# Where the gate and up weights lie in SBUF: one offset for every split buffer, and other homes for three blocks

## The chip, the core and the metric

The kernel runs on one core of one Trainium2 chip. The metric is the device time of the whole kernel in microseconds, the median of several executions. Engines are called as in the profile: PE is the matrix engine (PEld its weight loads), DVE the vector engine, ACT the scalar engine, POOL the general one and SP the one that issues most transfers.

## What is computed

One layer of a hybrid decoder on 512 tokens of width 1024, in float32. Two token mixers (a gated linear recurrence and a sparse attention with three branches) share one input projection, and a sandwich-normed feed-forward and a gated input embedding follow. The part that matters here is the feed-forward's first half:

```python
h = rmsnorm(x, norm_ffn_pre[i])
gate, up = jnp.split(h @ ffn_w_gate_up[i], 2, axis=-1)          # h: 512 x 1024, weights: 1024 x 5632
x = x + rmsnorm((jax.nn.silu(gate) * up) @ ffn_w_down[i], norm_ffn_post[i])
x = x + jax.nn.sigmoid(x @ ple_w_gate[i] + ple_b_gate[i]) * (p[i] @ ple_w_proj[i])
```

## The kernel before

**Products.** A float32 product is made of three matmuls on rounded operands: every operand is split into a high part (a cast on ACT) and a low part (a subtraction on DVE), and `three` adds high x high, high x low and low x high in one PSUM bank. The normed tokens lie transposed in `aTh` and `aTl`, 8 slices of 128 rows by 512 tokens. For every matmul PE loads a stationary operand of 128 x 128 and streams a moving one past it, and the load of the next one runs while the present one streams.

**The gate and up stage.** The 2816 columns of gate and of up are cut into 22 blocks of 128 (`NF`). A block needs its gate weights and its up weights, 128 x 1024 values each, as a high and a low tile. There are three forms.

- Blocks 0 and 1 (`first`) run in two halves of 256 tokens, because the last tokens are still being normed and transposed (`to_T`, L254 and L255). The up weights of block 1 have tiles of their own, `UP1`; the other three pairs lie in `whf` and `wlf`.
- Blocks 2, 3 and 4 (up to `SF` = 5) are plain: `gu_load` loads and splits, `gu_mm` runs 24 matmuls of 512 tokens for gate into bank `mm` and 24 for up into bank `sc`, `gu_act` applies the SiLU (L1224), multiplies (L1225), and splits and stores what the down-projection needs.
- Blocks 5 to 21 (`s_block`) use seven half-size products instead of eight, on sums of tokens (T1, T3, T2, T4, made once in `t_sums` while blocks 2 to 4 run, L1302 to L1312) and sums of weights (`s_load`, L1348 and L1349 for the splits). Each has seven stretches of 12 matmuls of 256 tokens: two with gate weights, two with w12, two with w34 and one with the high half of the up weights, vw. The weights of the first six lie in `whf` and `wlf`, those of the last in `vwh` and `vwl`, whose low part is finished by an adding transfer from POOL's queue (L1358).

**The buffers.** The pool `wp2` holds three loaded tiles (`rawf`), three `whf` and three `wlf`, used in turn. `wtile` cuts a tile of 1024 floats out of a buffer of 1024 + `STEP` floats, and small tiles named pad lie between the groups. SBUF is laid out in the order in which the tiles are first named, so a pad of n floats moves all that follows by 4n bytes. The pool `ff` opens behind it in the space of the out-projection's weights (`wo`) and norms, and holds a home for each tile of the feed-forward: `a0` to `a5` and `s0` to `s10` for the activations, the sums, w12 and w34, and `vwh`, `vwl`. A home can be written once whatever lay in its bytes, or in the same home before, was read for the last time. The weights that the attention stage reads are in another pool, opened and closed earlier; the attention pool `attn` begins with homes (`KS0` to `pc`), behind which small tiles and the scores' exponentials `e` follow; PE transposes `e` with the identity as the moving operand (`tr<-ident,e`).

**Order.** PE's matmuls keep the program's order in this stage (`strict`). The order of the other engines' instructions is set when the program is built, by priorities and estimated times; `wload` gives its load, cast and subtraction a priority of 100 places ahead (`AHEAD`). Each engine then runs its queue in that order, and an instruction that waits holds up those behind it.

Of the kernel before, what the change touches and what calls it, by code (L numbers as in the profile page):

```python
# [8 lines left out]
F32 = mybir.dt.float32  # L9
F32R = mybir.dt.float32r  # L10
# [6 lines left out]
S, D, KT, TT = 512, 1024, 8, 4  # L17
# [18 lines left out]
VP = (4,)  # L36

SF = 5
STEP = 16
SA = 160  # L40
WARM = 13
PTB = 3
# [2 lines left out]
def f32(ap):  # L45
    return ap.bitcast(F32)
# [3 lines left out]
def layer_kernel(ctx, tc, a, out):  # L50
# [14 lines left out]
    def nm(s):  # L65
        uid[0] += 1
        return f"{s}{uid[0]}"

    def bank(tag, shape=None):
        return ps.tile(shape or [128, 512], F32, tag=tag, name=nm(tag), bufs=PB[tag])  # L70
# [8 lines left out]
    def wraw(src, shape, w, ahead=None):  # L79
        raw = wpool[0].tile(shape, F32, tag="raw" + w, name=nm("raw"), bufs=WB[w][0])  # L80
        with tc.high_priority(offset=AHEAD if ahead is None else ahead):
            nc.sync.dma_start(raw, src)
        return raw

    def wtile(tag, shape=(KT, 128), dt=F32R):

        v = wpool[0].tile([128, KT * 128 + STEP], dt, tag=tag, name=nm(tag), bufs=WB["f"][1])[:, :KT * 128]
        return v.rearrange("p (k c) -> p k c", k=shape[0])

    def wload(src, shape, w, hl=None):  # L90

        raw = wraw(src, shape, w)
        h, l = hl or [wtile(x + w) for x in ("wh", "wl")]
        with tc.high_priority(offset=AHEAD):
            nc.scalar.copy(h, raw)
            nc.vector.tensor_sub(l, raw, f32(h))
        return h, l
# [654 lines left out]

    KS, QS, PTc, E, ATT = {}, {}, {}, {}, {}
    for tag, n, bufs in (("KS0", 4 * S, 1), ("KS1", 4 * S, 1), ("KS2", 4 * S, 1), ("QS", S, 6), ("PT", 2 * S, PTB),
                         ("pc", 2 * S, 1)):
        ap_.tile([128, n], F32, tag=tag, name=nm("home"), bufs=bufs)

    def k_epi(j, br):
# [307 lines left out]


    wpool[0] = ctx.enter_context(tc.tile_pool(name="wp2", bufs=2, reuse_waits="tile"))
    for tag, n, bufs in (("rawf", 1024, 3), ("pad0", 8, 1), ("whf", 1024 + STEP, 3), ("pad1", 16, 1),
                         ("wlf", 1024 + STEP, 3), ("pad2", 8, 1)):  # L1070
        wpool[0].tile([128, n], F32, tag=tag, name=nm("home"), bufs=bufs)
    late = ctx.enter_context(tc.tile_pool(name="late", bufs=1, reuse_waits="tile"))
# [79 lines left out]
            post1(t, 0, YP[t])  # L1152
    wgu = a["ffn_w_gate_up"][0].rearrange("(k p) c -> p k c", p=128)

    def gu_load(f, up=None):
        return (wload(wgu[:, :, f * 128:(f + 1) * 128], [128, KT, 128], "f"),
                wload(wgu[:, :, DFF + f * 128:DFF + (f + 1) * 128], [128, KT, 128], "f", up))

    with tc.issue_after(WO["dma", 3].ins):
        first = [gu_load(0)]  # L1160
# [8 lines left out]
    for ch in (1,):  # L1169
        ws = WO[ch]  # L1170
        for t in range(TT):
            p_ = bank(("pv", "mq")[t % 2])
            tl = slice(t * 128, (t + 1) * 128)
            three(p_, [(aTh[:, k, tl], aTl[:, k, tl], ws[k // 2][0][:, k % 2], ws[k // 2][1][:, k % 2])
                       for k in range(KT)],
                  {TK[0]: turn_0, TK[1]: turn_1} if t == TT - 1 else {})
            post1(t, ch, p_)
            resid(t, og, sss)
            norm2_sum(t)
            if t != 2:  # L1180
                norm2(t)
            if t == 1:
                first.append(gu_load(1, UP1))
# [19 lines left out]
    def gu_mm(w, banks, cs, then=None):  # L1203
        for i, ((wh, wl), p_) in enumerate(zip(w, banks)):
            three(p_[:, cs], [(wh[:, k], wl[:, k], aTh[:, k, cs], aTl[:, k, cs]) for k in range(KT)],
                  {TK[2]: then} if i == 1 and then else {})
# [45 lines left out]
    ff = ctx.enter_context(tc.tile_pool(name="ff", bufs=1, reuse_waits="tile"))  # L1252
# [3 lines left out]
    for j in range(NJ2):  # L1256
        if j == NJ2 - 1:
            for t_, n in (("t1", 8), ("t3", 8), ("t2", 8), ("tm", 4), ("w12", 4), ("w34", 4)):
                ff.tile([128, n * HS], F32, tag=t_, name=nm("home"))
            ff.tile([128, 56], F32, tag="pad0", name=nm("pad"))  # L1260
            for t_ in ("vwh", "vwl"):
                ff.tile([128, 2 * HS], F32, tag=t_, name=nm("home"), bufs=2)
            ff.tile([128, 8], F32, tag="pad1", name=nm("pad"))
        if j % 2 == 0:
            ff.tile([128, len(BLK[j // 2]), 2, HS], F32, tag=f"a{j // 2}", name=nm("home"))
        ff.tile([128, 2, 2, HS], F32, tag=f"s{j}", name=nm("home"))
# [22 lines left out]
    def t_sums(step):  # L1289

        if step == 0:
            SB["tmp"] = [home(t_, [128, half, HS], F32) for t_ in ("s8", "s9")]
        n_ = ("T1", "T3", "T2", "T4")[step]
        SB[n_] = part_of(0, 1)
        if step < 3:
            t_ = home(n_.lower(), [128, 2, half, HS])
            SB[n_] = t_[:, 0], t_[:, 1]
        x, z = SB["tmp"]
        lo1, lo2, hi1, hi2 = ([f32(v) for v in part_of(a_, b_)] for a_ in range(2) for b_ in range(2))

        def cut(n_, v):
            nc.scalar.copy(SB[n_][0], v)  # L1302
            nc.vector.tensor_sub(SB[n_][1], v, f32(SB[n_][0]))

        def diff(o_, t_, p_, q_):
            nc.vector.tensor_sub(o_, p_[0], q_[0])
            nc.vector.tensor_sub(t_, p_[1], q_[1])
            nc.vector.tensor_add(o_, o_, t_)

        def minus(o_, v, q_):  # L1310
            nc.vector.scalar_tensor_tensor(o_, v, -1.0, q_[0], op0=OP.mult, op1=OP.subtract)
            nc.vector.tensor_sub(o_, o_, q_[1])  # L1312

        if step == 0:
            diff(x, z, lo1, lo2)
            cut("T1", x)
        elif step == 1:
            diff(z, x, hi2, lo2)
            cut("T3", z)
        elif step == 2:  # L1320
            minus(x, z, lo1)
            cut("T2", x)
            minus(z, x, hi1)
        else:
            cut("T4", z)
# [54 lines left out]
    def s_block(f):  # L1380
        gw, w12, w34, vw = s_load(f)
        X, Z, W = (bank(t_)[:, :HS] for t_ in ("mm", "sc", "tr"))
        if f == SF:
            SB["tmp"] = home("tm", [128, half, HS], F32)
        P1, P5, U2, U3 = (SB["tmp"][:, i] for i in range(half))

        def times(p_, w, at, b, fresh=False):
            for k in range(half):
                for n_, (u, m_) in enumerate(((0, 0), (0, 1), (1, 0))):
                    mm(p_, w[u][:, at + k], b[m_][:, k], start=fresh and k == 0 and n_ == 0,  # L1390
                       stop=k == half - 1 and n_ == 2, skip_group_check=not fresh)

        def act(st, o_):
            times(X, gw, 0, part_of(0, 0), True)
            nc.scalar.copy(P1, X)
            times(W, gw, half, part_of(1, 0), True)
            nc.vector.tensor_add(st[:, :HS], W, P1)
            times(X, w12, half, SB["T2"])
            nc.scalar.copy(U2, X)
            times(Z, w12, 0, SB["T1"], True)  # L1400
            last["P5"] = nc.scalar.copy(P5, Z)
            times(X, w34, 0, SB["T3"])
            last["U3"] = nc.scalar.copy(U3, X)
            times(Z, w34, half, part_of(1, 1))
            nc.vector.tensor_add(st[:, HS:], Z, U2)
            last["silu"] = tab(nc.scalar.activation(st, st, AF.Silu))
            times(X, vw, 0, SB["T4"])
            nc.vector.tensor_add(U3, U3, P5)
            nc.vector.scalar_tensor_tensor(o_[:, :HS], X, -1.0, st[:, :HS], op0=OP.mult, op1=OP.mult)
            last["o2"] = nc.vector.scalar_tensor_tensor(o_[:, HS:], U3, -1.0, st[:, HS:], op0=OP.mult, op1=OP.mult)  # L1410

        gu_act(f, act, None)

    strict[0] = True
    for f in range(2, NF):
        if f - 2 <= SF - 2:
            t_sums(f - 2)
        if f >= SF:
            s_block(f)
            continue  # L1420
        w, banks = gu_load(f), (bank("mm"), bank("sc"))
        gu_mm(w, banks, slice(0, S))
        gu_act(f, *banks)

# [71 lines left out]
    for b, js in enumerate(BLK):  # L1496
        n, end = len(js), b == len(BLK) - 1
# [152 lines left out]
    for b, js in enumerate(BLK):  # L1650
        w, s4 = ws.pop(b)
# [115 lines left out]
```

## Time and profile before

| what | value |
|---|---|
| median of 3 executions | 896.84 us (896.24 to 896.94) |
| the profiled execution's own time | 896.88 us |
| its span from first to last instruction | 895.1 us |
| PE busy | 884.7 us, 99% |
| DVE busy | 705.4 us, 79% |
| ACT busy | 557.1 us, 62% |
| POOL busy | 161.1 us, 18% |
| gate and up stage, first to last matmul | 495.79 to 724.13 us of the span |

In the profile's groups, a line gives the operation, the tile written, the tiles read, and the shape. Matmuls overlap in the records: a matmul of 512 columns is shown as some 0.39 us long and one of 256 as 0.28, while the next one begins earlier; what a matmul costs in a dense stretch is the distance from its start to the next one's. L107 is the helper that issues every matmul, so tiles and start times tell the matmuls apart. In a timeline, a row is a start, a length, the engine, the line, the operation, the tiles, the shape and the number of instructions merged. In the chain of waits a row is a start, a length and what ran.

### The profile page before, as it was taken

The numbers are of one execution on the slowest core, as the hardware profiler recorded it, in microseconds if no ns is written. First come the engines' busy times: TensorE is split into PE (matmuls) and PEld (weight loads), VectorE is DVE, ScalarE is ACT, GpSimd is POOL, SyncE is SP. The second block draws the span as 40 slices with busy tenths as digits, with TensorE's granted clock in tenths as the row PEclk, the third lists the DMA queues.
The fourth block names the chain that finished last, engine by engine and source line by source line (L and its number), as shares of the span: only waits on it lengthen the run. The fifth ranks groups of instructions, "written<-read, shape, count | busy, mean of one in ns | idle before, by whom it ended". The sixth has DMA issues, their size and how long they took to land.

```text
span 895.1 us, 14187 instructions
## 1 busy us (share of the span) xinstructions
PE 884.7 (99%) x5111; PEld 761.9 (85%) x5111; DVE 705.4 (79%) x1366; ACT 557.1 (62%) x1072; POOL 161.1 (18%) x247
## 2 busy tenths in 40 slices
PE   8999999999999999999999999999999999999998
PEld 6977888878888888888888988999999988878887
DVE  6657786968788788787848589888888898898852
ACT  6468958666677667767736345676667664466520
POOL 4101201214143232323402100111111100002000
PEclk9999999999999999999999999999999999999999
DMA  9433435282114111111048244666667675558511
GB/s 299 98 95 98 115 95 165 74 162 71 41 44 107 48 48 48 47 48 48 26 140 258 94 123 125 147 164 166 151 146 182 159 222 192 191 181 245 189 59 48
DMA packets 138934, 110.94 MB, mean 124 GB/s; under 512 B 6936, under 2 KB 119664, under 8 KB 138864
## 3 DMA queue, kind: packets, MB, share of 16 engines
q1 hardware_dynamic: 126272, 95.61, 36.2%
q0 software_dynamic: 12576, 14.42, 8.1%
q8 instruction: 40, 0.66, 0.3%
q14 instruction: 30, 0.25, 0.1%
q10 hardware_dynamic: 16, 0.00, 0.0%
HBM read 97.96 MB, written 8.91 MB: 119 GB/s over the span
## 4 chain that ended last, share of the span: by engine, by line
PE 90%; DVE 5%; ACT 2%; issue 1%; DMA 1%; SPq 1%; POOL 0%; DVEq 0%; ACTq 0%
PE mm L107 47%; PE sc L107 19%; PE mq L107 7%; PE tr L107 6%; PE pv L107 5%; PE tr L110 4%; DVE wl L169 1%; DMA y<-in_w_in_dram 1%; DVE PT L953 1%; DVE e L862 1%; ACT e L865 1%; DVE aTl L1441 1%; PE sc L110 0%; ACT wh L168 0%; DVE QS L783 0%
## 5 line engine op out<-in xcount | busy, mean ns | idle before, releaser
L107 PE MATMUL mm<-aTh,wh 128*128 128x512 f32 x344 | 140.4, 408 | 0.0
L107 PE MATMUL mm<-aTh,wl 128*128 128x512 f32 x344 | 134.7, 392 | 0.0
L107 PE MATMUL mm<-aTl,wh 128*128 128x512 f32 x344 | 134.5, 391 | 0.0
L877 POOL TENSOR_SCALAR e<-e,sm 128x128 f32<-128x128 f32 (+3 forms) x128 | 78.8, 632 | 152.8 <-DVE sm L873 102.2
L169 DVE TENSOR_TENSOR wl<-raw,wh 128x1024 fp32r<-128x1024 f32 x59 | 73.5, 1249 | 25.6 <-ACT wh L168 21.1
L865 ACT ACTIVATE e<-e,mn 128x128 f32<-128x128 f32 (+3 forms) x128 | 71.5, 559 | 28.4 <-DVE mn L862 18.2
L168 ACT CAST wh<-raw 128x1024 fp32r<-128x1024 f32 x59 | 61.7, 1047 | 26.6 <-PE mm L107 23.7
L107 PEld LDWEIGHTS mm<-aTh,wl 128*128 128x128 f32 x344 | 64.6, 188 | 14.2
L107 PEld LDWEIGHTS mm<-aTh,wh 128*128 128x128 f32 x344 | 64.7, 188 | 12.9 <-issue 3.4
L107 PEld LDWEIGHTS mm<-aTl,wh 128*128 128x128 f32 x344 | 64.9, 189 | 9.4
L862 DVE CUSTOM_DVE_ANT_0 e<-sc,toep 128x128 f32<-128x128 f32 (+3 forms) x128 | 59.8, 484 | 16.0 <-PE sc L107 15.2
L953 DVE TENSOR_TENSOR PT<-tr,PT 128x512 fp32r<-128x512 f32 x96 | 56.6, 596 | 15.6 <-ACT PT L952 15.0
L952 ACT CAST PT<-tr 128x512 fp32r<-128x512 f32 x96 | 47.9, 512 | 24.5 <-PE tr L110 23.4
L1349 DVE TENSOR_TENSOR wlf<-T,whf 128x1024 fp32r<-128x1024 f32 x34 | 41.6, 1224 | 22.9 <-ACT whf L1348 22.9
L107 PE MATMUL sc<-KS,QS 128*128 128x512 f32 (+2 forms) x192 | 54.1, 364 | 0.1
L107 PE MATMUL mm<-T,whf 128*128 128x256 f32 x272 | 50.1, 282 | 0.0
L110 PE MATMUL tr<-ident,e 128*128 128x128 f32 x320 | 48.6, 272 | 0.0
L110 PEld LDWEIGHTS tr<-ident,e 128*128 128x128 f32 x320 | 39.9, 141 | 9.2 <-DVE PT L953 0.3
L107 PEld LDWEIGHTS mm<-T,whf 128*128 128x128 f32 x272 | 41.8, 188 | 0.0
L107 PE MATMUL mm<-T,aTh 128*128 128x512 f32 (+1 forms) x144 | 40.6, 367 | 0.0
L107 PEld LDWEIGHTS sc<-KS,QS 128*128 128x128 f32 x192 | 33.8, 188 | 7.9 <-issue 1.4
L1348 ACT CAST whf<-T 128x512 fp32r<-128x512 f32 x68 | 38.5, 616 | 1.5 <-PE sc L107 1.5
(462 smaller groups left out, 2507.1 us busy)
## 6 DMA issues: line engine op xcount, KB each, us to landing
raw<-in_w_in_dram SPq DMA_DIRECT2D x48, 512.0 KB, 3.8
raw<-in_ffn_w_gate_up_dram SPq DMA_DIRECT2D x44, 512.0 KB, 4.2
raw<-in_ffn_w_down_dram SPq DMA_DIRECT2D x25, 512.0 KB, 4.4
rd<-r POOLq DMA_DIRECT2D x11, 512.0 KB, 3.9
w<-in_ffn_w_gate_up_dram POOLq DMA_DIRECT2D x17, 256.0 KB, 5.2
raw<-in_ple_w_gate_dram SPq DMA_DIRECT2D x8, 512.0 KB, 4.6
x<-in_x_dram SPq DMA_DIRECT2D x7, 512.0 KB, 8.0
raw<-in_w_out_dram SPq DMA_DIRECT2D x6, 512.0 KB
```

The lines of the kernel that those rows point to most:

```text
L107: return pe(nc.tensor.matmul(*args, **kw))
L110: return pe(nc.tensor.transpose(*args))
L168: nc.scalar.copy(h, RAW[n])
L169: nc.vector.tensor_sub(l, RAW[n], f32(h))
L862: nc.vector.tensor_tensor_reduce(e[:, br, :], src, toep[:, 384 - 128 * i:S], SLOPE[h], BIG, op0=OP.add, op1=OP.min, accum_out=mn[:, u, br: ...
L865: tt(nc.scalar.activation(e[:, br, :], e[:, br, :], AF.Exp, scale=-1.0, bias=mn[:, u, br:br + 1], accum_out=sm[:, u, br:br + 1]))
L877: nc.gpsimd.tensor_scalar(ev, ev, sm[:, v, br:br + 1], 1.0, op0=OP.mult, op1=OP.mult)
L952: nc.scalar.copy(P[:, 0, :2 * n], pt[:, :2 * n])
L953: nc.vector.tensor_sub(P[:, 1, :2 * n], pt[:, :2 * n], f32(P[:, 0, :2 * n]))
L1348: last["cut"] = nc.scalar.copy(h[:, k:k + half], x[:, k:k + half])
L1349: nc.vector.tensor_sub(l, x, f32(h))
L1441: last["turn"] = fn(*args)
```

## The change

It changes where tiles lie, and no instruction's kind, size or number.

- `STEP` goes from 16 to 0, so the three `whf` buffers and the three `wlf` buffers are no longer 64 bytes apart modulo 256. `pad0` and `pad1` of the pool `wp2` grow to 56 and 64 floats. Every `whf` and `wlf` tile then starts 32 bytes below the tokens modulo 256. The pool's size stays the same.
- In the pool `ff`, `pad0` shrinks by 8 floats and `pad1` grows by 8: `vwh` and `vwl` go from 32 to 64 bytes below the tokens modulo 256, and what follows stays.
- Blocks 2, 3 and 4 take their split weights in homes that later hold activations: block 2 in s4 to s7, block 3 in s2, s3, a1 and a2, block 4 in a3, a4, and again s4 and s5. These are at the tokens' offset. Blocks 0, 1 and 5 to 21 share the `whf` and `wlf` buffers as before.
- In the attention pool a pad of 16 floats behind the homes moves all that follows by 64 bytes.

```diff
-STEP = 16
+STEP = 0
...
-                         ("pc", 2 * S, 1)):
+                         ("pc", 2 * S, 1), ("pad", 16, 1)):
...
-    for tag, n, bufs in (("rawf", 1024, 3), ("pad0", 8, 1), ("whf", 1024 + STEP, 3), ("pad1", 16, 1),
+    for tag, n, bufs in (("rawf", 1024, 3), ("pad0", 56, 1), ("whf", 1024 + STEP, 3), ("pad1", 64, 1),
                          ("wlf", 1024 + STEP, 3), ("pad2", 8, 1)):
...
-    def gu_load(f, up=None):
-        return (wload(wgu[:, :, f * 128:(f + 1) * 128], [128, KT, 128], "f"),
+    def gu_load(f, up=None, gate=None):
+        return (wload(wgu[:, :, f * 128:(f + 1) * 128], [128, KT, 128], "f", gate),
                 wload(wgu[:, :, DFF + f * 128:DFF + (f + 1) * 128], [128, KT, 128], "f", up))
...
-            ff.tile([128, 56], F32, tag="pad0", name=nm("pad"))
+            ff.tile([128, 48], F32, tag="pad0", name=nm("pad"))
             for t_ in ("vwh", "vwl"):
                 ff.tile([128, 2 * HS], F32, tag=t_, name=nm("home"), bufs=2)
-            ff.tile([128, 8], F32, tag="pad1", name=nm("pad"))
+            ff.tile([128, 16], F32, tag="pad1", name=nm("pad"))
...
     strict[0] = True
+    PLAIN = (("s4", "s5", "s6", "s7"), ("s2", "s3", "a1", "a2"), ("a3", "a4", "s4", "s5"))
     for f in range(2, NF):
         if f - 2 <= SF - 2:
             t_sums(f - 2)
         if f >= SF:
             s_block(f)
             continue
-        w, banks = gu_load(f), (bank("mm"), bank("sc"))
+        hl = [ff.tile([128, KT, 128], F32R, tag=t_, name=nm("w")) for t_ in PLAIN[f - 2]]
+        w, banks = gu_load(f, hl[:2], hl[2:]), (bank("mm"), bank("sc"))
         gu_mm(w, banks, slice(0, S))
```

## The prediction

> **What bounds the kernel now.** I read the page first, then the busy time of each engine by stage, then the chain of waits and the order of TensorE's matmuls inside the gate and up stage, which is the only stage the change's weights lie in.
>
> ```profile
> span 895.1 us, 14187 instructions
> PE 884.7 (99%) x5111; PEld 761.9 (85%) x5111; DVE 705.4 (79%) x1366; ACT 557.1 (62%) x1072; POOL 161.1 (18%) x247
> PE 90%; DVE 5%; ACT 2%; issue 1%; DMA 1%; SPq 1%; POOL 0%; DVEq 0%; ACTq 0%
> ```
>
> TensorE carries 90% of the chain that ended last, so what decides is how far apart its matmuls start. The stages (columns: stretch, its length, busy time and count for PE, PEld, DVE, ACT, POOL, then granted clock, DMA share, GB/s):
>
> ```profile
> 496.00:521.00 25.00, 24.91 (x209) 24.64 (x208) 12.39 (x17) 9.16 (x14) 3.32 (x5) 1.00 0.41 127
> 521.00:555.00 34.00, 34.00 (x148) 27.44 (x149) 32.05 (x42) 14.75 (x22) 2.43 (x3) 1.00 0.41 125
> 555.00:600.00 45.00, 45.00 (x382) 45.00 (x381) 39.23 (x67) 30.09 (x63) 6.26 (x6) 1.00 0.63 146
> ```
>
> The first row is blocks 0 and 1 (256-column halves), the second the three plain blocks 2 to 4 (512 columns), the third the first of the seventeen seven-product blocks (256 columns). PE has no gap in the last two, at full clock. VectorE has the least room in the plain stage, 32.05 of 34 us, and half its time free just before.
>
> **Where the buffers lie.** This comes from the sizes in the code. Ahead of the weights every tile is a whole number of 256 bytes, and tokens and sums (aTh, aTl, T) share one offset modulo 256; call it 0. Before: pad0 of 8 floats puts the first whf buffer at +32, and 1024+16 floats a buffer put the next two at +96 and +160; pad1 makes wlf the same. The last product's vwh and vwl stand behind 56 floats, so at 224, that is -32. After: whf and wlf all at -32 (56 floats, no step, 64 floats between), vwh and vwl at -64 (48 floats), blocks 2 to 4 in homes s4 to a4, which are at 0. In attention, e goes from -64 (six 32-byte tiles stand before it) to 0.
>
> **Term 1, the seventeen blocks.** TensorE's rows inside one block (start, length, then what it is) and at the end of the stage:
>
> ```profile
> 584.50 0.28 PE L107 MATMUL mm<-aTh,whf 128*128 128x256 f32 x1
> ...
> 588.78 0.40 PE L107 MATMUL sc<-T,whf 128*128 128x256 f32 x2
> ...
> 590.22 0.41 PE L107 MATMUL mm<-T,whf 128*128 128x256 f32 x2
> ...
> 593.07 0.28 PE L107 MATMUL mm<-aTh,w 128*128 128x256 f32 x1
> ...
> 594.48 0.28 PE L107 MATMUL mm<-aTh,whf 128*128 128x256 f32 x1
> ```
> ```profile
> 554.62 0.28 PE L107 MATMUL mm<-aTh,whf 128*128 128x256 f32 x1
> ```
> ```profile
> 724.13 0.63 PE L107 MATMUL mm<-whf,a 128*128 128x512 f32 x2
> ```
> ```profile
> 554.50:724.50 170.00, 26.61 (x204) 25.08 (x204) 0.00 (x0) 20.17 (x32) 20.42 (x16) 1.00 0.65 158
> ```
>
> The last row is the same kind of table for the instructions on tile w alone (vwh and vwl). Its 204 matmuls are 17 stretches of 12, each lasting 11 steps and one length of 0.28: 26.61/17 = 1.565, less 0.28, over 11 = 116.8 ns a step at -32. The whole stage is 724.13 - 554.62 = 169.51 us for 17 x 84 matmuls; take off 204 x 116.8 = 23.83, and the other 1224 stand at 145.68/1224 = 119.0 ns. The worst stretch (588.78 to 590.22, offset +160) is 120.0. These are the same instructions on the same shapes with nothing waited for, and they differ only by buffer. If all 1224 take the step that w takes: 1224 x (119.0 - 116.8) = **2.7 us less**. Bounds: nothing (the step stays 119.0) and, on the bad side, 1224 x (120.0 - 119.0) = 1.2 us more. I take 2.7, since -32 is a measured offset here.
>
> The 204 matmuls of w move to -64, which no matmul of 256 columns has in this trace. Its neighbours are -32 (116.8) and +160, which is -96 (120.0). Midway is 118.4: 204 x 1.6 = **0.3 us more**. Bounds: 204 x 3.2 = 0.7 more, and as far the other way, 0.7 less.
>
> **Term 2, the plain blocks.** Matmuls of 512 columns, at a nonzero offset (to 554.62, above) and at 0:
>
> ```profile
> 520.56 0.28 PE L107 MATMUL sc<-aTh,up 128*128 128x256 f32 x1
> 520.89 0.50 PE L107 MATMUL mm<-aTh,whf 128*128 128x512 f32 x1
> 521.23 0.40 PE L107 MATMUL mm<-aTl,whf 128*128 128x512 f32 x1
> ```
> ```profile
> 729.68 0.62 PE L107 MATMUL tr<-aTh,s 128*128 128x512 f32 x2
> ...
> 732.40 0.39 PE L107 MATMUL pv<-aTh,T 128*128 128x512 f32 x1
> ```
>
> The plain blocks take 554.62 - 520.89 = 33.73 us for 144, or 234.2 ns. Twelve matmuls between tiles at equal offsets take 2.72, or 226.7. At 0: 144 x 226.7 = 32.64, **1.1 us less** (0.1 of it is the late first one, 0.34 for 0.23). Bounds: 0.1, if the homes bring only that, and 1.1.
>
> The first plain block also starts late: 520.56 to 520.89 is 0.33 where a step is 0.12. The chain says why:
>
> ```profile
> 509.39 2.84 PE mm L107 x24
> 512.23 2.89 PE sc L107 x24
> 515.12 2.74 PE mm L107 x23
> ...
> 517.88 1.05 ACT whf L95
> ...
> 518.95 1.28 ACT L1224
> ...
> 520.24 0.61 ACT st L1224
> ```
>
> ScalarE casts block 3's gate weights as soon as block 1's gate matmuls free their buffer, and then loads the activation table and runs the SiLU that frees block 2's PSUM bank. With weights in homes that cast needs no buffer of block 1 and stands earlier; the SiLU follows block 0. **0.2 us less**. What is late next is block 2's up bank, which the product at L1225 frees, and it is not needed until 526.6. Bounds 0 and 0.2.
>
> **Term 3, blocks 0 and 1.** Three of their four buffers go to -32. The second half's three chain rows are 2.84 + 2.89 + 2.74 x 24/23 = 8.59 us for 72, 119.3 ns; both halves, 144 x (119.3 - 116.8) = **0.4 us less** (bounds 0 and 0.4). The fourth, UP1, stays at 0.
>
> **Term 4, edits at nothing.** The pads add up to the same 512 bytes in the weight pool and 64 floats in the ff pool, so nothing else moves. No instruction is added: six casts, six subtractions and six loads write elsewhere. Subtractions do not mind the offset (min, median, max over buffers at +32, +96, +160):
>
> ```profile
> L1349 DVE TENSOR_TENSOR wlf<-raw,whf x17: 1218/1224/1229, 544.9 to 708.3; 128x1024 fp32r<-128x1024 f32 x17
> ```
>
> That is why I price no write. The e tiles' transposes, at -64 now, against those of xn, at 0:
>
> ```profile
> 228.39 1.03 PE L110 MATMUL tr<-ident,e 128*128 128x128 f32 x8
> ```
> ```profile
> 489.12 1.03 PE L110 MATMUL tr<-ident,xn 128*128 128x128 f32 x8
> ```
>
> Both are 1.03 for eight, so the 64 bytes are worth nothing; the rounding of 0.01 on each of 40 such groups bounds it at 0.4 either way.
>
> **Term 5, order.** This is the edit that can cost. The splits of blocks 2 and 3 now wait only for out-projection weights (last read at 495.56) and loads. They can enter ScalarE's and VectorE's queues among the norm and transposes of tokens 2 and 3, whose readers are these:
>
> ```profile
> 496.10 0.19 PEld L107 LDWEIGHTS mm<-aTl,whf 128*128 128x128 f32 x1 [0.35 <-DVE aTl L255]
> ```
> ```profile
> 502.62 1.28 DVE L1115 SCALAR_TENSOR_TENSOR xn<-x,rstd,g 128x1024 f32<-128x1024 f32 x1 [0.66 <-POOL rstd L242]
> 503.82 0.68 DVE L255 TENSOR_TENSOR aTl<-tr,aTh 128x512 fp32r<-128x512 f32 x1
> 507.10 1.29 DVE L255 TENSOR_TENSOR aTl<-tr,aTh 128x512 fp32r<-128x512 f32 x2 [2.60 <-ACT aTh L254]
> ```
>
> The last aTl ends at 508.39; the second half, which reads it, starts one step before 509.35, at 509.23: cover 0.8 us. One split (1.23 on VectorE) in front costs 0.4; in front of the aTl at 496.10, with no cover, up to 1.2. In return the plain stage loses two to four of its subtractions, 2.4 to 4.9 of VectorE's 32.05 us, and so stays under PE's shorter 32.6. I take nothing, as VectorE idles 2.6 us before 507.10 and 4.8 after it, and keep 1.6 (both places) for the range.
>
> **Sum.** 2.7 - 0.3 + 1.1 + 0.2 + 0.4 = 4.1 less. Each block keeps VectorE at 39.23 of 45 us where PE then needs 44.3, so no other engine takes over. In the down-projection the waits are for VectorE,
>
> ```profile
> PE tr L107 <- DVE aTl L1441: 0.8, 2, 0.5
> ```
>
> and its queue there starts from the last block's products, so it shifts along. The profiled execution took 896.88 against a median of 896.84, so both bases agree: 896.9 - 4.1 = **892.8 us**.
>
> **Rivals.** *Buffer, not offset.* The low step of w comes from something else about its tiles, and whf stays at 119.0. For: w is the only tile at -32 with 256 columns. Against: the steps differ between whf's own three buffers (120.0 at worst, 118 to 119 at 584.50 to 588.78). Terms 1 and 3 go, 1.3 stay: 895.6.
>
> *Nothing moves but the wait.* Operand offsets do not matter to TensorE, and the spacing comes from sequence alone. Then only the late start goes, 0.3: 896.6. Against it stand 234.2 and 226.7 ns for one shape. The Trainium skill, SBUF — State Buffer, section "Who interferes with whom", gives TensorE two independent SBUF read ports, one for the moving operand and one for weight loads, and says that it never waits on anyone. By that rule this rival would hold; the rows disagree with it, by 3% at 512 columns, and I follow the rows.
>
> *One or two splits in the way.* Term 5 at 1.6: 894.4.
>
> *Slower: the splits ahead of the last token tile.* If all six subtractions stand on VectorE ahead of xn at 502.62, the second half is late by 6 x 1.23 - 0.8 = 6.6, and PE waits at the first matmul of that half. 892.8 + 6.6 = 899.4. It decides from four splits on (4.9 - 0.8 = 4.1 cancels the gain). Against it: three raw buffers hold only three loads, and block 4's up weights reuse homes of block 2's gate, which PE reads until 526.
>
> **How the numbers follow.** Forecast 0.64, one or two splits 0.13, buffer not offset 0.13, nothing but the wait 0.05, slower 0.05. A measurement of this kernel can tell about 0.2%, or 1.8 us: faster means under 895.05. Forecast and splits lie there, 0.77; the two offset rivals lie within, 0.18; slower 0.05. The range goes from 891.4 (w at its good bound, 1.0 below, and e's 0.4) to 895.7, which takes in the splits and the buffer rival.
>
> **What would show it.** Right: w's and whf's steps near 117 ns, a block of 84 near 9.83 us instead of 9.97, plain blocks at 226.7 ns, no late start at block 2, ScalarE's six casts at L95 from 496 on, e's transposes still 1.03. Wrong: whf's step at 119 or over; a PE wait between 494 and 510 of more than a microsecond; a new wait in the down-projection that grows by what the blocks saved.

## The result and the profile after

The changed kernel takes 891.23 us (median of 6, 890.65 to 891.73) against 896.89 us before (median of 6, 896.24 to 898.22): a ratio of 0.9936, 95% interval 0.9923 to 0.9949, so 5.66 us or 0.63% less, and the interval leaves out 1. The forecast was 892.8 us, in a range from 891.4; the kernel is 1.6 us faster than forecast and 0.2 us below that range. The profiled execution took 890.65 us, the fastest of the six.

The page of the changed kernel: span, TensorE's busy time, and the engines' shares of the chain that ended last.

```profile
span 888.9 us, 14177 instructions
...
PE 878.5 (99%) x5111; PEld 757.8 (85%) x5111; DVE 704.8 (79%) x1366; ACT 556.4 (63%) x1072; POOL 159.8 (18%) x247
...
PE 91%; DVE 4%; ACT 2%; issue 1%; DMA 1%; SPq 1%; POOL 0%; DVEq 0%; ACTq 0%; POOLq 0%
```

TensorE bounds it as before, with the same 5111 matmuls and 6.2 us less busy time. The first of the seven-product blocks again (stretch, its length, busy time and count for PE, PEld, DVE, ACT, POOL, then granted clock, DMA share, GB/s), and below them the instructions on tile w alone, which now holds the plain blocks' weights too until 552:

```profile
555.00:600.00 45.00, 45.00 (x390) 45.00 (x389) 38.61 (x67) 31.94 (x67) 6.26 (x6) 1.00 0.63 153
```
```profile
554.50:724.50 170.00, 25.94 (x204) 24.37 (x204) 0.00 (x0) 20.18 (x32) 20.42 (x16) 1.00 0.67 166
```

No engine took over: VectorE is busy 38.61 of 45 us in the seven-product blocks, and PE has no gap at full clock. The last row gives w's step as the prediction read it: 25.94/17 = 1.526, less 0.28, over 11 = 113.3 ns at offset -64, where before it was 116.8 at -32.

The chain through the stage (start, length, what ran) shows the rest. A row of 12 or 24 matmuls is a stretch, and its length over its count is the step.

```profile
508.39 2.80 PE mm L107 x24
511.20 2.80 PE sc L107 x24
514.00 2.81 PE mm L107 x24
516.80 2.88 PE sc L107 x24
519.68 5.47 PE mm L107 x24
525.14 5.44 PE sc L107 x24
...
552.35 1.40 PE mm L107 x12
```
```profile
609.55 2.76 PE mm L107 x24
612.31 1.40 PE tr L107 x12
...
617.91 1.40 PE sc L107 x12
619.31 2.76 PE mm L107 x24
```

The second half of blocks 0 and 1 at -32 takes 2.80/24 = 116.7 ns, with only UP1 at offset 0 left at 2.88/24 = 120.0. The plain blocks take 5.44/24 = 226.7. A seven-product block is 619.31 - 609.55 = 9.76 us: each stretch of whf 1.40/12 = 116.7, and the 2.76 is one stretch of w at 1.36 and one of gate weights at 1.40.

The ScalarE cast and the table load that sat in front of block 2's PSUM bank are gone from the chain. TensorE at block 2, then ScalarE's rows:

```profile
519.39 0.28 PE L107 MATMUL sc<-aTh,up 128*128 128x256 f32 x1
519.51 0.40 PE L107 MATMUL mm<-aTh,w 128*128 128x512 f32 x1
```
```profile
506.44 2.96 ACT L95 CAST w<-raw 128x1024 fp32r<-128x1024 f32 x3
509.41 1.28 ACT L1224 ACT_TABLE_LOAD   x1
511.23 0.60 ACT L1224 ACTIVATE st<-mm 128x512 f32<-128x512 f32 x1 [0.54 <-PE mm L107]
```

Block 2 starts 0.12 us, one step, behind its neighbour, where it was 0.33. Three casts run at 506.44, and the table load stands at 509.41 where it was at 518.95.

Where the 6.23 us between the two profiled executions went, from the starts of the first matmul of each stage (495.79, 520.89, 554.62, 724.13 and the last one at 890.65 before; 494.92, 519.51, 552.19, 718.11 and 884.42 after):

| stage | before, us | after, us | less, us | forecast, us |
|---|---|---|---|---|
| ahead of the gate and up stage | 495.79 | 494.92 | 0.87 | 0 |
| blocks 0 and 1, with the late start | 25.10 | 24.59 | 0.51 | 0.6 |
| plain blocks | 33.73 | 32.68 | 1.05 | 1.1 |
| seventeen seven-product blocks | 169.51 | 165.92 | 3.59 | 2.4 |
| behind | 166.52 | 166.31 | 0.21 | 0 |

Two questions follow. Is a step that falls with an offset a matter of the offset alone? And is the 0.87 us ahead of the stage the work of the pad in the attention pool?

### The profile page after: what moved, and what is told of

The parts are those of the page before. It is cut to its first block, busy times and chain, and to the rows that moved or that the text cites. A ratio compares the mean times of both kernels' runs of the same rounds, so it can differ in the third digit from the quotient of the medians.

```text
span 888.9 us, 14177 instructions
## 1 busy us (share of the span) xinstructions
PE 878.5 (99%) x5111; PEld 757.8 (85%) x5111; DVE 704.8 (79%) x1366; ACT 556.4 (63%) x1072; POOL 159.8 (18%) x247
## 4 chain that ended last, share of the span: by engine, by line
PE 91%; DVE 4%; ACT 2%; issue 1%; DMA 1%; SPq 1%; POOL 0%; DVEq 0%; ACTq 0%; POOLq 0%
PE mm L107 48%; PE sc L107 20%; PE mq L107 7%; PE tr L107 6%; PE pv L107 6%; PE tr L110 4%; DVE wl L169 1%; DMA y<-in_w_in_dram 1%; ACT e L865 1%; DVE PT L953 1%; DVE aTl L1443 1%; PE sc L110 0%; ACT PT L952 0%; ACT wh L168 0%; DVE e L862 0%
## 5 line engine op out<-in xcount | busy, mean ns | idle before, releaser
L107 PE MATMUL mm<-aTh,wh 128*128 128x512 f32 x344 | 140.4, 408 | 0.0
L107 PE MATMUL mm<-aTh,wl 128*128 128x512 f32 x344 | 134.5, 391 | 0.0
L107 PE MATMUL mm<-aTl,wh 128*128 128x512 f32 x344 | 134.5, 391 | 0.0
L107 PEld LDWEIGHTS mm<-aTh,wl 128*128 128x128 f32 x344 | 64.6, 188 | 14.3
L107 PEld LDWEIGHTS mm<-aTh,wh 128*128 128x128 f32 x344 | 64.7, 188 | 12.9 <-issue 3.4
L107 PEld LDWEIGHTS mm<-aTl,wh 128*128 128x128 f32 x344 | 64.9, 189 | 9.4
L107 PE MATMUL sc<-KS,QS 128*128 128x512 f32 (+2 forms) x192 | 54.0, 363 | 0.0
L107 PE MATMUL mm<-T,whf 128*128 128x256 f32 x272 | 49.1, 279 | 0.0
L110 PE MATMUL tr<-ident,e 128*128 128x128 f32 x320 | 48.6, 272 | 0.0
L110 PEld LDWEIGHTS tr<-ident,e 128*128 128x128 f32 x320 | 39.8, 140 | 9.0 <-DVE PT L953 0.3
L107 PEld LDWEIGHTS mm<-T,whf 128*128 128x128 f32 x272 | 41.4, 188 | 0.0
L107 PE MATMUL mm<-aTh,w 128*128 128x256 f32 (+1 forms) x184 | 41.2, 306 | 0.0
L107 PE MATMUL mm<-T,aTh 128*128 128x512 f32 (+1 forms) x144 | 40.5, 367 | 0.0
L107 PEld LDWEIGHTS sc<-KS,QS 128*128 128x128 f32 x192 | 33.9, 188 | 7.3 <-issue 0.8
```

What stands on the lines that cost most here:

```text
L107: return pe(nc.tensor.matmul(*args, **kw))
L110: return pe(nc.tensor.transpose(*args))
```

## The experiments

All of them compute the whole result. In the table, the offsets are those of the seven-product blocks' gate weights, w12, w34 and w, in bytes from the tokens modulo 256; the "plain" column is the offset of blocks 2 to 4, and the lengths come from matmul starts in one profiled execution each. Block is a seven-product block from the third on. Each ratio is against the kernel before on the same chip, whose medians lay between 896.64 and 896.89 us.

| kernel | offsets | plain | median, us | ratio to before (95%) | blocks 0, 1 | plain | seventeen | block |
|---|---|---|---|---|---|---|---|---|
| before | 32, 160, 96, -32 | 32 to 160 | 896.89 | 1 | 25.10 | 33.73 | 169.51 | 9.973 |
| after | -32, -32, -32, -64 | 0 | 891.23 | 0.9936 (0.9923-0.9949) | 24.59 | 32.68 | 165.92 | 9.760 |
| e1 | all -64 | 0 | 893.31 | 0.9959 (0.9947-0.9972) | 24.33 | 32.67 | 168.18 | 9.893 |
| e2 | all -32 | 0 | 891.88 | 0.9945 (0.9933-0.9958) | 24.61 | 32.68 | 166.60 | 9.800 |
| e3 | as after | 0 | 891.16 | 0.9936 (0.9922-0.9949) | 24.58 | 32.68 | 165.92 | 9.760 |
| e4 | as before | 0 | 895.26 | 0.9982 (0.9973-0.9991) | 24.86 | 32.67 | 169.47 | 9.973 |
| e5 | -32, -64, -64, -64 | 0 | 888.75 | 0.9909 (0.9895-0.9922) | 24.75 | 32.67 | 163.20 | 9.600 |
| e6 | 0, 0, 0, -64 | 0 | 895.88 | 0.9988 (0.998-0.9997) | 25.01 | 32.67 | 169.99 | 10.000 |
| e7 | as after | -32 | 894.09 | 0.9967 (0.9956-0.9977) | 24.86 | 33.71 | 168.11 | 9.893 |
| e8 | 64, -64, 128, -64 | 64, -64, 128 | 893.44 | 0.9964 (0.9952-0.9977) | 24.91 | 33.48 | 166.67 | 9.698, 9.922 |
| e9 | -64, -64, -64, -32 | 0 | 893.33 | 0.9962 (0.995-0.9974) | 24.40 | 32.67 | 168.18 | 9.893 |
| e10 | all -32 | -32 | 893.8 | 0.9966 (0.9954-0.9978) | 24.83 | 33.71 | 166.60 | 9.800 |
| e11 | e7 again | -32 | 894.7 (one) | | 24.81 | 33.71 | 168.11 | 9.893 |
| e12 | all -64, first block's gate 0 | 0 | 888.04 | 0.9902 (0.9886-0.9919) | 24.45 | 32.67 | 161.99 | 9.520 |
| e13 | as e12 | 0 | 888.0 | 0.99 (0.9884-0.9917) | 24.39 | 32.67 | 161.99 | 9.520 |

### The parts one by one: e2, e3, e4

**e2: w back at -32.**

```diff
-            ff.tile([128, 48], F32, tag="pad0", name=nm("pad"))
+            ff.tile([128, 56], F32, tag="pad0", name=nm("pad"))
...
-            ff.tile([128, 16], F32, tag="pad1", name=nm("pad"))
+            ff.tile([128, 8], F32, tag="pad1", name=nm("pad"))
```

> The changed kernel with vwh and vwl back at -32. Theory: w's 204 matmuls go from 113.3 back to 116.8 ns and the time up by 0.7 us, to 891.9. Rival (w was quick for another reason, such as the homes' order): no step changes, 891.2.

Measured: 891.88 us, 0.65 more than the changed kernel. The row of tile w, as above:

```profile
554.50:724.50 170.00, 26.56 (x204) 25.05 (x204) 0.00 (x0) 20.22 (x32) 20.42 (x16) 1.00 0.67 164
```

26.56/17 less 0.28 over 11 is 116.6 ns, and the seventeen blocks take 166.60 - 165.92 = 0.68 us more. So w's move from -32 to -64, which the forecast put down as a cost, is a gain of 0.7 us.

**e3: no pad in the attention pool.**

```diff
-                         ("pc", 2 * S, 1), ("pad", 16, 1)):
+                         ("pc", 2 * S, 1)):
```

> The changed kernel without the pad in the attention pool, so e at -64 again. The profiled execution of the changed kernel was 0.6 us ahead by the end of attention beyond its lead at 18 us. Theory (e's offset is worth it): 0.3 to 0.6 us more, 891.5 to 891.8, and the lead at the start of the out-projection shrinks by as much. Rival (that lead is the spread of executions): 891.2, and the starts in the attention stage differ no more than at its beginning.

Measured: 891.16 us, the same as with the pad. The stage's first matmul in this execution, then a group of e's transposes in the changed kernel:

```profile
496.13 0.28 PE L107 MATMUL mm<-aTh,whf 128*128 128x256 f32 x1
```
```profile
227.63 1.03 PE L110 MATMUL tr<-ident,e 128*128 128x128 f32 x8
```

The start of the stage does not follow the pad: it lies at 495.41 (e4) and 496.13 (e3) without it, and anywhere from 494.92 (the changed kernel) to 497.23 (e7) with it. So the 0.87 us ahead of the stage is within what executions differ by, and no worth of the pad shows.

**e4: the kernel before, with the plain blocks' weights in homes and nothing else.**

```diff
+    PLAIN = (("s4", "s5", "s6", "s7"), ("s2", "s3", "a1", "a2"), ("a3", "a4", "s4", "s5"))
...
-        w, banks = gu_load(f), (bank("mm"), bank("sc"))
+        hl = [ff.tile([128, KT, 128], F32R, tag=t_, name=nm("w")) for t_ in PLAIN[f - 2]]
+        w, banks = gu_load(f, hl[:2], hl[2:]), (bank("mm"), bank("sc"))
```

> The kernel before with only blocks 2 to 4 in homes. Theory: the plain blocks take 32.64 instead of 33.73 us and start without the 0.2 us wait; all else stays: 1.3 us less than before, 895.6. Rival (the homes' gain is the freed buffers for the first seven-product blocks, or nothing): 234 ns a matmul stays, 896.7.

Measured: 1.38 us less than before by the medians (896.64 and 895.26). In the trace it is 0.24 in blocks 0 and 1 with the late start, and 1.06 in the plain blocks, 1.30 in all. The chain now runs on through block 2, and its rows are the changed kernel's:

```profile
517.55 2.88 PE sc L107 x24
520.43 5.47 PE mm L107 x24
```

### Is the step a matter of the offset? e1, e6, e8

**e1: whf and wlf at -64 too, where w had 113.3.**

```diff
-    for tag, n, bufs in (("rawf", 1024, 3), ("pad0", 56, 1), ("whf", 1024 + STEP, 3), ("pad1", 64, 1),
-                         ("wlf", 1024 + STEP, 3), ("pad2", 8, 1)):
+    for tag, n, bufs in (("rawf", 1024, 3), ("pad0", 48, 1), ("whf", 1024 + STEP, 3), ("pad1", 64, 1),
+                         ("wlf", 1024 + STEP, 3), ("pad2", 16, 1)):
```

> All split buffers of the seven-product blocks at -64 (whf, wlf and w alike); blocks 2 to 4 in homes as in the changed kernel. Theory (the offset sets the step): the 1224 matmuls of whf and wlf in the seven-product blocks go from 116.7 ns to w's 113.3 at -64, so a block of 84 takes 9.52 us instead of 9.76, 17 blocks 4.1 us less, and blocks 0 and 1 0.5 less: near 886.6 us. Rival (it is w's place in memory, not its offset): whf stays at 116.7 and the time at 891.2.

Measured: 893.31 us, 2.1 more than the changed kernel. The chain in a block:

```profile
610.18 2.83 PE mm L107 x24
613.01 1.41 PE tr L107 x12
```

Every stretch stands at 2.83/24 = 117.9 ns (9.893/84 = 117.8 over a block), and w, whose address is the same as in the changed kernel, has gone from 113.3 to 117.8 with them. The offset alone does not set the step.

**e6: whf and wlf at 0, in the same buffers.**

```diff
-    for tag, n, bufs in (("rawf", 1024, 3), ("pad0", 56, 1), ("whf", 1024 + STEP, 3), ("pad1", 64, 1),
-                         ("wlf", 1024 + STEP, 3), ("pad2", 8, 1)):
+    for tag, n, bufs in (("rawf", 1024, 3), ("pad0", 64, 1), ("whf", 1024 + STEP, 3), ("pad1", 64, 1),
+                         ("wlf", 1024 + STEP, 3)):
```

> The changed kernel with whf and wlf at the tokens' own offset, 0. Theory (the offset of the same buffers sets the step): 120 ns for the 1224 matmuls as every 256-column matmul at 0 had before, so 1224 x 3.3 = 4.0 us more, and 144 x 3.3 = 0.5 in blocks 0 and 1: 895.7. Whether w at -64 behind a stretch at 0 takes 113.3 or 117.8 is open. Rival (the step belongs to place or sequence): 891.2.

Measured: 895.88 us, 4.65 more than the changed kernel. The chain in a block:

```profile
612.29 2.80 PE mm L107 x24
615.09 1.44 PE tr L107 x12
```

The stretches of whf take 1.44/12 = 120.0 ns, and 2.80 - 1.44 = 1.36 is w at 113.3. Same instructions in the same buffers moved by 32 bytes, 3.3 ns a matmul: so the offset does set the step, but not alone.

**e8: three other offsets, one a buffer, and no homes.**

```diff
-STEP = 0
+STEP = 16
...
-    for tag, n, bufs in (("rawf", 1024, 3), ("pad0", 56, 1), ("whf", 1024 + STEP, 3), ("pad1", 64, 1),
-                         ("wlf", 1024 + STEP, 3), ("pad2", 8, 1)):
+    for tag, n, bufs in (("rawf", 1024, 3), ("pad0", 16, 1), ("whf", 1024 + STEP, 3), ("pad1", 16, 1),
+                         ("wlf", 1024 + STEP, 3)):
...
-        w, banks = gu_load(f, hl[:2], hl[2:]), (bank("mm"), bank("sc"))
+        w, banks = gu_load(f), (bank("mm"), bank("sc"))
```

> No homes, and the three whf and wlf buffers at +64, +128 and -64: the offsets that no run has yet, for 256 and for 512 columns. Theory (only offset 0 is free of delay at 512 columns, and each nonzero offset has its own step at 256): 231 to 236 ns at 512 columns at all three, and between 113.3 and 120 at 256. Rival (some of them are free too): 226.7 at 512 columns at one of them.

Measured: 893.44 us. The two stretches of w12 in the chain (bank sc is the second of them), the second of one block and both of the next, with a stretch of gate weights (bank tr) ahead of these:

```profile
607.36 1.42 PE sc L107 x12
...
614.40 1.36 PE tr L107 x12
615.76 1.36 PE mm L107 x12
617.12 1.36 PE sc L107 x12
```

w12 at -64 takes 1.42 in one block (at 607.36) and 1.36 in the next (615.76, 617.12), by the same instructions on the same addresses of w12 and of the tokens. The blocks alternate between 9.922 and 9.698 us from the second to the seventeenth. At the same offset there are two rhythms. By this run alone the sequence need not be what settles them: from block to block the products also change between two places for tile w and between two PSUM banks for each of mm, sc and tr. They do so in the other kernels too, whose blocks do not alternate (9.760 us each in the changed kernel). The gate weights at +64 also take 1.36 (at 614.40), so -64 is not the only offset that reaches 113.3. At 512 columns none of the three is free of delay: in the same chain a step is 228.8 and 229.6 ns at -64, 232.1 and 233.3 at +128 and 233.3 at +64, against 226.7 at 0. So the rival falls, but -64 lies below the 231 to 236 of the theory.

### What settles the rhythm? e5, e7, e9, e10, e11

The theory from here on: at -64 and at -32 there is a fast and a slow rhythm, what runs just before decides, and a rhythm then lasts.

**e5: gate weights at -32, the rest at -64.** The buffers of `whf` and `wlf` get a tag each, used in the same turn.

```diff
-    for tag, n, bufs in (("rawf", 1024, 3), ("pad0", 56, 1), ("whf", 1024 + STEP, 3), ("pad1", 64, 1),
-                         ("wlf", 1024 + STEP, 3), ("pad2", 8, 1)):
+    for tag, n, bufs in (("rawf", 1024, 3), ("pad0", 48, 1), ("whf1", 1024, 1), ("whf2", 1024, 1),
+                         ("wlf1", 1024, 1), ("wlf2", 1024, 1), ("pad1", 8, 1), ("whf0", 1024, 1),
+                         ("wlf0", 1024, 1), ("pad2", 72, 1)):
```

> The changed kernel with gate weights of the seven-product blocks at -32 and w12, w34 and w at -64 (homes as in the changed kernel). All at -64 gave 117.8 ns a step, while w at -64 behind a stretch at -32 took 113.3. Theory (two rhythms at -64, and the offset before it chooses): each block enters -64 from -32 and stays at 113.3 for 60 matmuls; a block is 24 x 116.7 + 60 x 113.3 = 9.60 us against 9.76, 17 blocks 2.7 us less than the changed kernel: 888.5. Rival (113.3 lasts only a dozen steps, then falls to 117.8): about 9.82 a block, 892.2.

Measured: 888.75 us (888.56 to 888.81), 2.5 less than the changed kernel. The chain in a block (L110 is the helper that was L107, three lines on):

```profile
609.09 2.76 PE mm L110 x24
611.85 1.40 PE tr L110 x12
613.25 1.36 PE mm L110 x12
```

Behind gate weights at -32 (1.40), w12 and w34 at -64 run in the fast rhythm that they missed in e1. In the second half of blocks 0 and 1 of the same execution they do not. Block 0's gate weights at -32, then its up weights at -64:

```profile
508.84 2.80 PE mm L110 x24
511.64 2.83 PE sc L110 x24
```

Here -64 behind -32 takes 2.83/24 = 117.9. So the offset that ran just before does not decide alone.

**e9: the other way round, w at -32 and the rest at -64.** The edit is e1's and e2's together.

> Offsets swapped: whf and wlf at -64, and only w at -32 (homes as in the changed kernel). All at -64 took 117.8 ns a step in every block; 60 matmuls at -64 behind 24 at -32 took 113.3. Theory (a stretch at -32 brings the quick rhythm, and it lasts): from the second block on 72 x 113.3 + 12 x 116.7 = 9.56 us a block against 9.60 with gate at -32, 0.6 us less than that kernel: 888.1. Rival (12 matmuls at -32 are too few, or the entry from the slow rhythm at -64 does not lead out of it): 117.8 nearly throughout, 9.88 a block, 893.2.

Measured: 893.33 us, as e1. The row of tile w, and the chain at the second half of blocks 0 and 1, the end of the plain blocks and behind them:

```profile
554.50:724.50 170.00, 26.77 (x204) 25.23 (x204) 0.00 (x0) 20.17 (x32) 20.43 (x16) 1.00 0.66 163
```
```profile
514.13 2.72 PE mm L107 x24
516.85 2.88 PE sc L107 x24
...
546.96 5.44 PE sc L107 x24
552.39 1.41 PE mm L107 x12
```

w at -32 takes 26.77/17 less 0.28 over 11 = 117.7, slow as well, and its twelve do not lead back to the fast rhythm. But the same -64 is fast at 514.13, ahead of the plain blocks: 2.72/24 = 113.3. That half stands behind the first half's UP1, 256 columns at offset 0. It is slow once 512-column matmuls at offset 0 have run (552.39).

**e7: the changed kernel without the homes,** so that the plain blocks lie in whf and wlf at -32.

```diff
-        hl = [ff.tile([128, KT, 128], F32R, tag=t_, name=nm("w")) for t_ in PLAIN[f - 2]]
-        w, banks = gu_load(f, hl[:2], hl[2:]), (bank("mm"), bank("sc"))
+        w, banks = gu_load(f), (bank("mm"), bank("sc"))
```

> The changed kernel without the homes: blocks 2 to 4 in whf and wlf at -32 as in its other blocks. Theory: 234 ns for the 144 matmuls of 512 columns, 1.1 us, and the 0.2 us wait at block 2 is back: 892.5. Rival (the homes bring only the freed wait): 891.4, with 226.7 ns a step at -32.

Measured: 894.09 us (891.53 to 896.29), 2.9 more than the changed kernel. In the profiled execution, at 896.29 us the longest of the eleven, the plain blocks take 1.03 more and the seventeen blocks 2.19 more, though not one of the seventeen blocks' instructions or addresses differs. **e11** is the same kernel once more, for its wide spread:

> The same kernel as the one without homes, profiled once more. Theory (two rhythms of one program, chosen by where the first seven-product blocks are entered): this execution may show the other, 116.7 and 113.3 ns a step and blocks of 9.76 us, if its time is near 892.8; blocks of 9.89 if it is near 895.5. Rival (the rhythm is fixed by the layout): blocks of 9.89 us whatever the time, and the spread of its runs comes from the stages before.

Measured: 894.7 us, with the same block lengths to 0.001 us (9.815 for the first, then 9.893). The chain of e11 from the late start to the first two blocks:

```profile
519.85 0.61 ACT st L1224
...
526.37 5.60 PE sc L107 x24
...
561.37 1.40 PE sc L107 x12
562.78 2.83 PE mm L107 x24
565.60 1.41 PE tr L107 x12
```

The late start is back, the plain step is 5.60/24 = 233.3, the first block's six stretches at -32 run at 1.40, then w at -64 comes in slow, and everything behind it, at -32 too, is slow (1.41). The 1.6 us between these two executions lie almost wholly ahead of the stage, which starts at 497.23 in e7 and at 495.70 in e11.

That the layout alone settles the rhythm is not shown by this. Both profiled executions are slow ones. The eleven times of e7 spread over 4.8 us, where those of no other changed kernel spread over more than 2.2. Five of them, from 891.53 to 893.07, have a mean of 892.7, and 892.5 was expected without a slow rhythm. None of the five was profiled, so whether they ran in the fast rhythm stays open. At the start of the stage the executions do differ: the second twelve matmuls of block 0's gate weights, at -32 and at the same addresses in six profiled executions, take 116.7 ns a step in the changed kernel, e3 and e10, and 117.8 in e2, e7 and e11.

**e10: e7 with w at -32,** so that no -64 is there to lead into the slow rhythm.

> No homes, and whf, wlf, vwh and vwl all at -32. The kernel without homes and with w at -64 went over to 117.8 ns at -32 as well after its first stretch at -64, and its runs spread over 4.8 us. Theory (that slow rhythm at -32 is entered from -64, and only there): all at -32 the step stays at 116.7 in every block, as it did with homes: 1.1 + 0.2 for the homes and 0.7 for w over the changed kernel, 893.2, with a spread of no more than 2 us. Rival (the plain blocks at -32 themselves lead into 117.8): 117.8 from the first block on, 894.7.

Measured: 893.8 us, blocks of 9.800, all stretches at 116.7:

```profile
614.58 1.40 PE tr L107 x12
```

So in this execution, behind the plain blocks at -32, the step of 116.7 lasts with no stretch at -64 to end it. Beside e2 (plain blocks in homes, the same offsets otherwise) it takes 1.03 more in the plain blocks and 0.22 in blocks 0 and 1, the size of the homes by themselves.

### The entry alone: e12, e13

**e12: e1, but with the gate weights of the first seven-product block at 0,** in homes s6 and s7: 24 of the stage's 1428 matmuls read at another offset.

```diff
-        def cut(x):
-            h, l = (wtile(t_) for t_ in ("whf", "wlf"))
+        def cut(x, hl=None):
+            h, l = hl or [wtile(t_) for t_ in ("whf", "wlf")]
...
-            gw = cut(g)
+            gw = cut(g, [ff.tile([128, KT, 128], F32R, tag=t_, name=nm("w")) for t_ in ("s6", "s7")] if f == SF else None)
```

> As in the run with every weight at -64, but for the gate weights of the first seven-product block, which lie in homes s6 and s7 at offset 0: 24 matmuls of 256 columns. Theory (the step at -64 is set by what ran just before it, and then stays): 24 steps of 120.0 in that block, and all that follows at -64 takes 113.3 instead of 117.8, because the stretch of 12 at -64 behind matmuls of 256 columns at 0 did so in the run with whf and wlf at 0. 60 + 16 x 84 = 1404 steps, 4.5 ns less each, 6.3 us, and 0.05 more for the 24: 893.3 - 6.3 = 887.0 us, a block of 9.52 us. Rival (the fast rhythm holds only as long as something at -32 or 0 renews it in every block): the first block is faster by 0.2 to 0.3, the other sixteen stand at 117.8 and 9.893: 893.0 us. Second rival (what counts is the plain blocks of 512 columns before): 117.8 from the first stretch at -64 on, 893.3 us.

Measured: 888.04 us (887.12 to 888.53), 5.3 less than e1 and 3.2 less than the changed kernel. The chain from the last plain block on, and in a later block:

```profile
547.85 5.44 PE sc L107 x24
553.29 1.43 PE mm L107 x12
554.73 1.44 PE tr L107 x12
556.16 1.36 PE mm L107 x12
```
```profile
611.93 1.36 PE tr L107 x12
```

The 24 at 0 take 1.44/12 = 120.0, slower than anything in e1's seventeen blocks, and all 1404 behind them take 113.3: seventeen blocks in 161.99 us, where e1 took 168.18. That is 6.19 less, where 6.3 was expected. The sixteen later blocks are the same instructions at the same offsets in both kernels, at 9.893 and 9.520 us. The time is 1.0 us above the expected 887.0. Most of that lies ahead of the stage, which starts at 496.01 here and at 495.08 in e1, and 0.2 behind it; this was not followed further.

**e13: e12 with the turn of the buffers as in e1.** In e12 the two homes took no buffer out of the turn, so every later tile lay 4096 bytes on. Here the skipped buffers are claimed by copying two columns into them, and exactly the 24 read other addresses than in e1.

```diff
+            if f == SF:
+                for t_ in ("whf", "wlf"):
+                    nc.vector.tensor_copy(wtile(t_)[:, 0, :2], g[:, 0, :2])
```

> The run before it moved more than the 24 matmuls of the first block's gate weights: since these took no buffer out of the turn, every later tile lay one buffer (4096 bytes) further on than in the run with everything at -64, at the same offset. Here two columns are copied into the buffers that are skipped, so that the turn is the same, and exactly 24 of the 5091 matmuls read other addresses than in the run with everything at -64. Theory (the entry sets the rhythm): blocks of 9.520, the seventeen in 162.0 us, 887 to 888.5 us. Rival (the turn of the buffers did it): 117.8 ns and 9.893 from the first stretch at -64 on, 893.3 us.

Measured: 888.0 us (887.38 to 888.6), blocks of 9.520 and seventeen in 161.99 as in e12. A row of the chain in a later block:

```profile
612.47 1.36 PE tr L107 x12
```

1404 matmuls have the instructions, order and addresses of e1, the seventeen blocks are 6.19 us shorter, and the only difference on TensorE is where the 24 ahead of the 1404 read. The slow rhythm is no occasional stall: step by step, the 1404 take 117 to 119 ns in e1 and 113 or 114 here. All four times of e13, 887.38 to 888.6, lie below all five of e1, 892.96 to 893.85. With these layouts the entry sets the rhythm.

## Why the prediction was right and where it failed

- **What bounds it.** Right: TensorE's step set the time in every run, and no other engine became the bound.
- **Term 1, whf and wlf.** The number was right in the changed kernel: 9.760 us less 12 steps of 113.3 is 8.40 for 72, 116.7 ns, where 116.8 was forecast and 119.0 stood before. The reason was not: the forecast took this step to belong to -32 alone, and e7 and e9 show 117.8 at -32. In the changed kernel the blocks are entered from the homes in the faster rhythm, which the forecast did not ask about, so in this part it was lucky.
- **Term 1, w at -64: the step that failed.** "Midway is 118.4: 204 x 1.6 = 0.3 us more." It measured 113.3, a gain of 204 x (116.8 - 113.3) = 0.7 us; e2 gives 0.7 back. That is 1.0 us beyond the sum's term, and just the "as far the other way" bound. The range's low end allowed this 1.0 and 0.4 more for e; the measured time lies another 0.2 below. The error was to interpolate between offsets: steps over offsets are no smooth curve. At -32, -64 and 0 they are 116.7, 113.3 and 120.0 where each runs in its better rhythm. Nor did the forecast ask whether a step measured at an offset can change with what runs before it, which e1 shows: with whf and wlf at -64 as well, w at its same place takes 117.8.
- **Term 2.** Right: the plain blocks 1.05 for 1.1, and the late start gone; e4 has both alone, 1.30 in the trace for 1.3. What the term left out is that the homes also decide the rhythm of the blocks behind them, another 2.19 us with w at -64 (e7 and e11, in the profiled executions); with w at -32 it is nothing (e10 and e2, 166.60 us each).
- **Term 3.** Right: the second half's three rows are 2.80 + 2.80 + 2.81 = 8.41 us for 8.59, 0.18 less, so 0.36 if the first half gave as much. Over both halves it was 0.3: the 0.51 of the table less the 0.21 of the late start, where 0.4 was forecast.
- **Term 4.** Right: e3 shows no worth in the pad, e's transposes still take 1.03 for eight, and the subtractions 1224 ns:

```profile
L1349 DVE TENSOR_TENSOR wlf<-T,whf x34: 1215/1224/1226, 548.6 to 708.8; 128x1024 fp32r<-128x1024 f32 x34
```

- **Term 5.** Right to take nothing. VectorE's rows at the last token tile of the changed kernel: the idle time ahead of aTl is 2.51 us where it was 2.60, and three of the moved splits stand behind it, at 508.44:

```profile
501.70 1.28 DVE L1115 SCALAR_TENSOR_TENSOR xn<-x,rstd,g 128x1024 f32<-128x1024 f32 x1 [0.66 <-POOL rstd L242]
...
506.10 1.29 DVE L255 TENSOR_TENSOR aTl<-tr,aTh 128x512 fp32r<-128x512 f32 x2 [2.51 <-ACT aTh L254]
...
508.44 3.49 DVE L96 TENSOR_TENSOR w<-raw,w 128x1024 fp32r<-128x1024 f32 x3
```

  With that the rival of splits in the way and the slower one fall: no split stands ahead of xn at 501.70. One sign was off: ScalarE's casts were to run from 496 on, and the first of them runs at 506.44, behind the last cast of tokens, which is also why nothing was in the way.
- **The down-projection** kept its waits, as forecast, `PE tr L107 <- DVE aTl L1443: 0.9, 2, 0.5` (the same statement, as the code above it is two lines longer).
- **The sum.** 4.1 with w's term set right is 5.1; the medians give 5.66. The 0.5 left is not the stage's, which took 5.15 us less in the profiled execution (0.51 + 1.05 + 3.59). Ahead of the stage executions differ by more than 0.5 (it starts at 494.92 here and at 496.13 in e3), and no run shows a cause.
- **Buffer, not offset.** Fell with e6: the same buffers, 32 bytes on, took 120.0 for 116.7.
- **Nothing moves but the wait.** Fell with e4, e6 and e13. This rival leaned on the Trainium skill, SBUF — State Buffer, section "Who interferes with whom", by which PE's read ports for moving and stationary operands are independent and PE waits on nobody. The runs disagree with a spacing that follows from that rule: e1 and e13 differ in the addresses of 24 stationary operands on TensorE and by 6.19 us in that stage. Whether it is the two ports that are not independent, no run shows.

What stays open is the mechanism. The runs show which layouts led into which rhythm in the profiled executions; what in TensorE's reads or weight loads holds a rhythm over 1404 matmuls was not shown, nor what starts it beyond the entries tried here. The tokens lie at one place modulo 256 in every run, so it is also not shown whether the distance to them counts or the weights' own place.

## What to carry to other kernels

Where TensorE is dense, measure the step from start to start for every pair of operand offsets, stretch by stretch, and read it in the final sequence: a step measured elsewhere in a kernel is only a candidate. Try several layouts rather than interpolate, and look at the first stretch behind a change of shape, since it can decide the rest of a stage: here 24 matmuls at a slower offset bought 6.19 us. Where the times of one kernel spread as widely as those of e7, profile a short execution and a long one before calling a rhythm the kernel's own. An edit that looks local (other homes for three blocks) can move the blocks behind it as well.

## What the runs showed of the hardware beyond that

- The least step seen at 256 columns, 113.3 ns, is half of the 226.7 at 512 columns. At 512 columns only offset 0 reached 226.7; -32 gave 5.60/24 = 233.3 (e11) and -64 228.8 (e8). At 256 columns offset 0 is among the slowest, 120.0 (e6), and 113.3 was reached at -64 and, in every second block of e8, at +64.
- The step at -64 and what ran just before it: 113.3 behind 256 columns at 0 (w in e6, the entry in e12 and e13, and the second half of blocks 0 and 1 behind UP1 in e1, e9, e12 and e13); 117.8 behind 512 columns at 0 (e1, e9). Behind 256 columns at -32 it goes both ways: 113.3 in the seven-product blocks of the changed kernel and e5, entered from plain blocks at 0; 117.8 in those of e7 and e11, entered from plain blocks at -32, and in the second half of e5's blocks 0 and 1.
- From the third block on a rhythm repeats to within 0.004 us a block (e8, which alternates, against the block after next), and in e7 and e11 it was the same in both profiled executions, beside matmul spans that the records show alike (0.28 us).
